# The first and the refilled channel tiles of a two-layer decoder step: order and queues of the start, and one more plain tile in three half layers

## The chip, the core and the metric

The kernel runs on one core of a Trainium2 chip. Its engines are TensorE (in the profile PE for the products and PEld for the weight loads, which overlap them), VectorE (DVE), ScalarE (ACT), GpSimd (POOL) and SyncE (SP). Each takes its instructions in order and waits for others through semaphores. DMAs are issued by SP, ACT and POOL. The metric is the device time of one launch in microseconds (us), as the median of several runs.

## What is computed

The reference is one inference step of a two-layer decoder, for a prompt of 512 tokens and for 8 sample tokens, which the kernel treats as 520 columns that share the weights. Model width D is 1024 (8 channel tiles of 128), the inner width of a feed-forward half is 2816 (22 tiles of 128).

```python
def _swiglu(x, wg, wu, wd):
    return (jax.nn.silu(x @ wg) * (x @ wu)) @ wd
# every layer: x += 0.5*SwiGLU(rms(x)); x += mixer(rms(x)); x += 0.5*SwiGLU(rms(x))
```

The mixer of layer 0 is a causal pooling with four window sizes, that of layer 1 a windowed attention with sinks on keys and values projected once after layer 0. Everything is float32. There are four SwiGLU halves: 0 and 1 around the pooling, 2 and 3 around the attention. They take most of the time.

## The kernel before

**Products in three terms.** A float32 operand is split into a high part in the rounded type of TensorE and the rest: ScalarE writes the high part (`wh`, `xh`, `th`, `hh`), VectorE the rest (`wl`, `xl`, `tl`, `hl`). `mm` (line 406) makes one product of a 128-channel tile as three terms, each in two halves of 260 columns: six matmuls. Weights are stationary, activations move.

**A half layer** is `ffn` (line 556). It walks its 22 inner tiles in parts of 8, 8 and 6. For each tile it makes the gate and the up product, and after each part the down products of that part, which are added to x. A tile is made in one of two ways:

- `plain_tile` (line 463): gate and up over 8 channel tiles, in four weight pieces of four channel tiles: 4 pieces x 4 channel tiles x 6 = 96 matmuls. VectorE makes four `wl`, and three more operations at the end (lines 488, 490 and 243).
- `strassen_tile` (line 499): the same result by seven instead of eight block products, `product` (line 428) at line 435: 7 x 4 x 3 = 84 matmuls. It wants seven weight pieces, two of them sums that VectorE makes (lines 161 and 165) and two accumulated by DMAs that GpSimd issues (lines 155 and 156). And it wants eight more pairs `tt` of sums of channel tiles, made once per half layer by `sums` (line 533), a generator of eight steps.

`NPL` (line 30) says how many tiles at the head of each half layer are plain: 3, 2, 2, 2.

**Hooks.** At the head of a half layer the norm of x isn't known yet. `start_hooks` (line 610) lists what is to be slipped in between: one or two empty hooks, `norm` (the sum of squares over `acc`, line 378, the inverse root on VectorE, and the first step of `sums`), an empty one, `norm_all` (the root spread over all partitions, line 395, then the end of tiles that waited for it), and seven more steps of `sums`: 12 hooks in halves 0 and 1, 11 in half 3. A plain tile takes one hook after each of its four pieces; what is left when the first Strassen tile comes is done all at once ahead of it. Half 2 has six hooks of its own.

**Order.** The kernel is written for a framework that plans each engine's order by a simulated timeline. `later` (line 248) pins an instruction behind the one written before it on its engine; what isn't pinned may be moved. `Weights` (line 95) is the queue of weights: `chunk` is one load into one of three raw buffers, `piece` one split of 128x512; `get` splits the next piece, `prefetch` splits up to five pieces ahead, `load` and `begin` issue the loads, on SP. There are six buffers for split pieces and four double banks of PSUM (`duo`).

**The start** (lines 628 to 676). ACT issues six small loads (gains in five pieces into `grow`, the samples) and two blocks of x; SP issues the other six blocks of x between the first weights. TensorE transposes the 72 gains (line 657) and the samples of all eight channel tiles (line 662), then per channel tile four blocks of x into PSUM (line 666). VectorE or ScalarE copies them into `x[k]` (lines 667, 669, 671), then the pair `xh`, `xl` is made (lines 245, 246). None of the transposes, copies and splits is pinned. The squares of x follow (lines 363 and 367), and `ffn` for half 0 makes its first tile as any other plain tile, piece by piece.

The functions that the change touches, with what calls them:

Of the kernel before, what the change touches and what calls it, by code (L numbers as in the profile page):

```python
# [11 lines left out]
F32 = mybir.dt.float32  # L12
# [8 lines left out]
KT = 8  # L21
# [5 lines left out]
H = TOK // 2  # L27
PARTS = (8, 8, 6)
LAG = 2
NPL = (3, 2, 2, 2)  # L30
HD = 64
NB = SP // P
WINS = (2, 4, 8, 16)
# [61 lines left out]
class Weights:  # L95
# [81 lines left out]
    def _split(self, i):  # L177
        nc = self.nc
        while self.ns <= min(i, len(self.items) - 1):
            it = self.items[self.ns]  # L180
            self.load(it[0])
            self.add_up(it[0])
            src = it[1](self.chunks[it[0]][1])
            n = src.shape[1]
            wh = self.splp.tile([P, 4, P], F32R, tag="wh", name="wh")
            wl = self.splp.tile([P, 4, P], F32R, tag="wl", name="wl")
            dh, dl = wh[:, :n, :], wl[:, :n, :]
            if len(src.shape) == 4:
                dh = dh.rearrange("p k (e d) -> p k e d", e=2)
                dl = dl.rearrange("p k (e d) -> p k e d", e=2)  # L190
            nc.scalar.activation(dh, src, AF.Copy)  # L191
            nc.vector.tensor_tensor(dl, src, dh.bitcast(F32), op=ALU.subtract)  # L192
# [17 lines left out]
def yoco_step(ctx, tc, ins, outs):  # L210
# [18 lines left out]
    def ps():  # L229
        return duo()[:, 0, :]  # L230
# [17 lines left out]
    def later(ins):  # L248

        return tc.keep_in_program_order(ins)  # L250
# [152 lines left out]
    def terms(w, xx):  # L403
        return ((w[0], xx[0]), (w[0], xx[1]), (w[1], xx[0]))

    def mm(w, kk, mov, banks, first, last, halves=(0, 1)):

        for i, (a, b) in enumerate(terms(w, mov)):
            for hf in halves:
                T.matmul(  # L410
                    banks[:, hf, :H],
                    a[:, kk, :],
                    hcols(b, hf),
                    start=(first and i == 0),
                    stop=(last and i == 2),
                )

    def mm_tile(mov, banks, prefetch=True):
        nk = len(mov)
# [43 lines left out]
    def plain_tile(tmp, mov, hs, hooks):  # L463

        pg, pu = duo(), duo()
        for k0 in (0, 4):
            for banks in (pg, pu):
                w = W.get()
                W.prefetch()
                for k in range(k0, k0 + 4):  # L470
                    mm(w, k - k0, mov[k], banks, k == 0, k == KT - 1)
                if hooks:
                    hooks.pop(0)()
        g = tmp.tile([P, TOK], F32, tag="g", name="g")
        t = tmp.tile([P, TOK], F32, tag="t", name="t")
        if not there[0]:
            S.copy(halves(g), pg[:, :, :H])
            S.copy(halves(t), pu[:, :, :H])

            def rest():  # L480
                V.tensor_tensor(g, g, R, op=ALU.mult)
                S.activation(g, g, AF.Silu)
                V.scalar_tensor_tensor(g, t, -1.0, g, op0=ALU.mult, op1=ALU.mult)
                hidden(g, hs)

            copied.append(rest)
        else:
            V.tensor_tensor(halves(g), pg[:, :, :H], halves(R), op=ALU.mult)
            S.activation(t, g, AF.Silu)
            V.scalar_tensor_tensor(halves(g), pu[:, :, :H], -1.0, halves(t), op0=ALU.mult, op1=ALU.mult)  # L490
            hidden(g, hs)
# [61 lines left out]
            split(tt[k + 4], t34)  # L553
            yield

    def ffn(fi, tmp, mov, hooks, tt, tags, after, before_last=None):
# [70 lines left out]

    mov1 = []
    with ff_pool() as tmp:
        grow = tmp.tile([72, P], F32, tag="g", name="grow")  # L630
        nc.scalar.dma_start(grow[0:48, :], norm_g.rearrange("l n (k p) -> (l n k) p", p=P))
        xs = [big.tile([NS, 512], F32, tag=t, name="xs") for t in HH]
        for i in range(2):
            nc.scalar.dma_start(xs[i], x_sample[:, 0, i * 512 : (i + 1) * 512])
        nc.scalar.dma_start(grow[48:56, :], kv_norm_g.rearrange("(k p) -> k p", p=P))
        nc.scalar.dma_start(grow[56:64, :], final_norm_g.rearrange("(k p) -> k p", p=P))
        nc.scalar.dma_start(grow[64:72, :], pool_scale.rearrange("l (k p) -> (l k) p", p=P))
# [4 lines left out]
        xv = x_prompt[0].rearrange("(b p) c -> p b c", p=P)  # L642

        xt = {}
        for c in range(4):
            for b2 in range(2):
                xt[c, b2] = big.tile([P, 2, 256], F32, tag=TT[b2], name="xt")
                eng = nc.scalar if b2 and c < 2 else nc.sync
                later(eng.dma_start(xt[c, b2], xv[:, 2 * b2 : 2 * b2 + 2, c * 256 : (c + 1) * 256]))
            if c in (0, 2):  # L650
                W.begin(2)
        W.load(2)
        mov0, tt = [], {}
        for k in range(KT):
            if k == 0:
                pg = duo()
                T.transpose(pg[:, 0, :72], grow, ident[:72, :72])
                S.copy(gT, pg[:, 0, :72])
                px = pg[:, 1, :]
                for i in range(KT):  # L660
                    o = px[:, i * NS : (i + 1) * NS]
                    T.transpose(o, xs[i // 4][:, (i % 4) * P : (i % 4 + 1) * P], ident[:NS, :NS])
            pk = ps()
            for b in range(NB):
                src = xt[k // 2, b // 2][:, b % 2, (k % 2) * P : (k % 2 + 1) * P]
                T.transpose(pk[:, b * P : (b + 1) * P], src, ident)
            V.tensor_copy(x[k][:, SP:TOK], px[:, k * NS : (k + 1) * NS])
            if k % 2:
                V.tensor_copy(x[k][:, 0:SP], pk)
            else:  # L670
                S.copy(x[k][:, 0:SP], pk)
            z = pair(XX, [P, TOK])
            split(z, x[k], gcol(0, k))
            mov0.append(z)
        for k in range(KT):
            square(k, tmp, "g")

        prep = {}
        sel = cp.tile([P, 34], F32, name="sel")
# [43 lines left out]
                if i % 2:  # L723
                    yield

        ffn(0, tmp, mov0, start_hooks(tmp, 0, tt, 2), tt, HH, deferred(1, tmp, "g", XX, mov1, TW), pool_prep())

    with tc.tile_pool(name="pm", bufs=2) as pm:
        for k in range(KT):
# [591 lines left out]
```

## Time and profile before

| What | Value |
|---|---|
| median of three runs | 1728.08 us |
| lowest and highest | 1722.71 and 1731.19 us |
| the profiled execution, whole | 1729.8 us |
| its span, from the first to the last instruction | 1728.0 us |
| PE busy | 1669.6 us (97%) |
| DVE busy | 1269.1 us (73%) |
| ACT busy | 904.7 us (52%) |
| POOL busy | 146.1 us (8%) |

All durations below come from the profiled execution; its whole time is 1.8 us above its span and 1.7 us above the median. In a row of the timeline the first two numbers are the start and the length in us, then engine, line, operation, what is written and read, how many instructions are merged in the row, and in brackets how long the engine was idle ahead of them and what ended that. A merged row of matmuls ends later than its last issue, since matmuls overlap; the pace is read from the starts. A row of the chain of waits has start, length, engine, tile, line and count. A row of a window has its bounds and length, then busy us and instructions of PE, PEld, DVE, ACT and POOL, the granted TensorE clock, the busy share of the DMA engines and the GB/s that they moved.

### The profile page before, as it was taken

What the parts mean: (1) busy time and instruction counts of PE and PEld (TensorE: products, weight loads), DVE (VectorE), ACT (ScalarE), POOL (GpSimd) and SP (SyncE); (2) the same over time, 40 slices, a digit from 0 to 9 for tenths busy, and PEclk for the clock granted to TensorE, in tenths of its full rate; (3) what the DMA queues carried; (4) which work ended last, traced back from release to release, by engine and by line L of the source; (5) the groups of instructions that cost most, each with busy time, mean ns of one, the idle gap of its engine ahead of it and who ended that gap; (6) DMA issues with size and microseconds to landing.
All of it is one profiled execution on the core that took longest, in us unless ns stands there. A gap on an engine that the chain in (4) does not pass through costs nothing.

```text
span 1728.0 us, 34367 instructions
## 1 busy us (share of the span) xinstructions
PE 1669.6 (97%) x13701; PEld 1654.0 (96%) x13701; DVE 1269.1 (73%) x2454; ACT 904.7 (52%) x1810; POOL 146.1 (8%) x178
## 2 busy tenths in 40 slices
PE   7999999999899999999999999998889999999996
PEld 7999999999899999999999999998779899999996
DVE  6966866877875875887866866878756785785765
ACT  6643634656552643655543634647855653462553
POOL 0101101001001101001101101100000110110100
PEclk9999999999999999999999999999979999999998
DMA  8646746663445845546646746642112465666531
GB/s 204 159 129 141 171 135 144 180 183 75 102 141 132 182 134 135 141 128 145 155 127 141 174 135 141 155 140 50 25 35 73 111 163 144 146 150 159 135 86 51
DMA packets 315872, 227.06 MB, mean 131 GB/s; under 512 B 9265, under 2 KB 290969, under 8 KB 315671
## 3 DMA queue, kind: packets, MB, share of 16 engines
q1 hardware_dynamic: 285872, 174.82, 35.5%
q0 software_dynamic: 23200, 41.82, 14.7%
q10 hardware_dynamic: 6638, 8.23, 1.5%
q8 instruction: 107, 1.75, 0.4%
q14 instruction: 55, 0.44, 0.1%
HBM read 180.89 MB, written 5.04 MB: 108 GB/s over the span
## 4 chain that ended last, share of the span: by engine, by line
PE 67%; DVE 4%; ACT 3%; issue 0%; ACTq 0%; DVEq 0%
PE ps L435 35%; PE ps L410 30%; ACT sm L1034 1%; DVE sm L1019 1%; PE ps L1075 1%; DVE wl L192 1%; PE ps L1159 0%; PE ps L1052 0%; DVE xl L243 0%; ACT xh L242 0%; PE ps L1127 0%; DVE rp L856 0%; ACT wh L191 0%; PE ps L1250 0%; ACT oT L1087 0%
## 5 line engine op out<-in xcount | busy, mean ns | idle before, releaser
L191 ACT ACTIVATE wh<-raw 128x512 fp32r<-128x512 f32 (+1 forms) x742 | 449.6, 621 | 542.8 <-PE ps L410 326.3
L192 DVE TENSOR_TENSOR wl<-raw,wh 128x512 fp32r<-128x512 f32 (+1 forms) x742 | 491.0, 677 | 206.9 <-ACT wh L191 202.2
L435 PE MATMUL ps<-th,wh 128*128 128x260 f32 x1264 | 358.4, 284 | 5.4 <-ACT th L242 3.7
L435 PE MATMUL ps<-tl,wh 128*128 128x260 f32 x1264 | 358.7, 284 | 0.4 <-DVE tl L243 0.4
L435 PE MATMUL ps<-th,wl 128*128 128x260 f32 x1264 | 356.5, 283 | 0.6 <-DVE wl L192 0.5
L410 PE MATMUL ps<-hh,wh 128*128 128x260 f32 x1376 | 282.1, 286 | 4.0 <-DVE mx L1019 3.0
L410 PE MATMUL ps<-hl,wh 128*128 128x260 f32 x1376 | 280.9, 284 | 0.0
L410 PE MATMUL ps<-hh,wl 128*128 128x260 f32 x1376 | 279.4, 283 | 0.0
L435 PEld LDWEIGHTS ps<-th,wh 128*128 128x128 f32 x1264 | 238.9, 189 | 6.7 <-ACT th L242 4.1
L435 PEld LDWEIGHTS ps<-tl,wh 128*128 128x128 f32 x1264 | 239.4, 189 | 1.3 <-DVE tl L243 1.3
L435 PEld LDWEIGHTS ps<-th,wl 128*128 128x128 f32 x1264 | 238.6, 189 | 1.0 <-DVE wl L192 1.0
L410 PEld LDWEIGHTS ps<-hh,wh 128*128 128x128 f32 x1376 | 213.4, 190 | 5.4 <-DVE mx L1019 3.6
L410 PEld LDWEIGHTS ps<-hl,wh 128*128 128x128 f32 x1376 | 215.0, 190 | 0.0
L410 PEld LDWEIGHTS ps<-hh,wl 128*128 128x128 f32 x1376 | 214.0, 189 | 0.0
L435 PE MATMUL ps<-xh,wh 128*128 128x260 f32 x708 | 198.9, 283 | 0.6 <-ACT wh L191 0.6
L435 PE MATMUL ps<-xl,wh 128*128 128x260 f32 x708 | 198.6, 283 | 0.0
L435 PE MATMUL ps<-xh,wl 128*128 128x260 f32 x708 | 194.7, 282 | 1.0 <-DVE wl L192 1.0
L156 POOL DMA_DIRECT2D raw<-raw x79 | 68.4, 866 | 1389.1 <-DVE wl L192 504.7
L589 DVE TENSOR_TENSOR u<-ps,R 128x520 f32<-128x520 f32 x96 | 67.0, 698 | 107.5 <-PE ps L410 107.5
L435 PEld LDWEIGHTS ps<-xh,wh 128*128 128x128 f32 x708 | 133.6, 189 | 1.0 <-ACT wh L191 0.8
L435 PEld LDWEIGHTS ps<-xl,wh 128*128 128x128 f32 x708 | 133.5, 189 | 0.0
L435 PEld LDWEIGHTS ps<-xh,wl 128*128 128x128 f32 x708 | 131.4, 189 | 1.4 <-DVE wl L192 1.4
(237 smaller groups left out, 2845.7 us busy)
## 6 DMA issues: line engine op xcount, KB each, us to landing
raw<-in_ffn_w_gate_dram SPq DMA_DIRECT2D x87, 512.0 KB, 4.1
raw<-in_ffn_w_up_dram SPq DMA_DIRECT2D x87, 512.0 KB, 5.4
raw<-in_ffn_w_down_dram SPq DMA_DIRECT2D x32, 1024.0 KB, 4.9
raw<-raw POOLq DMA_DIRECT2D x79, 256.0 KB, 3.3
S<-in_ffn_w_up_dram SPq DMA_DIRECT2D x79, 256.0 KB, 5.5
S<-raw POOLq DMA_DIRECT2D x79, 256.0 KB, 4.6
raw<-in_ffn_w_down_dram SPq DMA_DIRECT2D x16, 768.0 KB, 6.2
raw<-in_w_q_dram SPq DMA_DIRECT2D x8, 512.0 KB, 6.7
```

The lines of the kernel that those rows point to most:

```text
L156: G.dma_start(blk(raw, 2, 1), blk(raw, 1, 1), accum_op=ALU.add)
L191: nc.scalar.activation(dh, src, AF.Copy)
L192: nc.vector.tensor_tensor(dl, src, dh.bitcast(F32), op=ALU.subtract)
L410: T.matmul(banks[:, hf, :H], a[:, kk, :], hcols(b, hf), start=(first and i == 0), stop=(last and i == 2),)
L435: T.matmul(bank[:, :H], a[:, kk, :], b, start=(not more and kk == 0 and i == 0), stop=(kk == 3 and i == 2), skip_group_check=more,)
L589: V.tensor_tensor(halves(u), banks[m][:, :, :H], halves(R), op=ALU.mult)
L1019: V.tensor_tensor_reduce(out=sm[:, e * 256 : (e + 1) * 256], in0=self.pe[e][:, bi * 256 : (bi + 1) * 256], in1=cst[:, mk : mk + 256], op0= ...
L1034: S.activation(part(i), part(i), AF.Exp, bias=nm[:, i : i + 1], accum_out=den[:, i : i + 1])
L1075: T.matmul(po[:, bi * 256 : (bi + 1) * 256], a, p_[:, kc_], start=(n == 0), stop=(n == 3 * len(kts) - 1),)
```

## The change

It has two parts. **The start** is written anew. The loads are dealt out in a fixed order: ACT takes the gains of the six norms, the samples and the second quarter of x, SP the other three quarters and the weights, POOL the other gains (into a tile of their own, `grow2`, transposed after the squares). Twelve matmuls of ones by ones are issued at the very start, and a small Square on ScalarE. Then every channel tile is transposed, copied and split in an order that is pinned throughout, two channel tiles ahead of the products, and the gate and up products of the first tile are made per channel tile as it comes, not piece by piece. The first tile takes no hooks. **The plain tiles** become 4, 3, 2, 3 instead of 3, 2, 2, 2: so halves 0, 1 and 3 have one more, and in half 0 the first of the four is the one made in the start.

The diff, with the lists of loads shortened:

```diff
-NPL = (3, 2, 2, 2)
+NPL = (4, 3, 2, 3)
...
+        self.pin = lambda ins: ins
...
-            nc.scalar.activation(dh, src, AF.Copy)
-            nc.vector.tensor_tensor(dl, src, dh.bitcast(F32), op=ALU.subtract)
+            self.pin(nc.scalar.activation(dh, src, AF.Copy))
+            self.pin(nc.vector.tensor_tensor(dl, src, dh.bitcast(F32), op=ALU.subtract))
...
+        plain_end(tmp, pg, pu, hs)
+
+    def plain_end(tmp, pg, pu, hs):
+
         g = tmp.tile([P, TOK], F32, tag="g", name="g")
         t = tmp.tile([P, TOK], F32, tag="t", name="t")
...
-                if j < NPL[fi]:
+                if j == 0 and first is not None:
+                    plain_end(tmp, *first, hs)
+                elif j < NPL[fi]:
                     plain_tile(tmp, mov, hs, hooks)
...
+        grow = tmp.tile([48, P], F32, tag="g", name="grow")
+        grow2 = tmp.tile([24, P], F32, tag="g", name="grow2")
+        later(nc.scalar.dma_start(grow, norm_g.rearrange("l n (k p) -> (l n k) p", p=P)))
         xs = [big.tile([NS, 512], F32, tag=t, name="xs") for t in HH]
         for i in range(2):
+            later(nc.scalar.dma_start(xs[i], x_sample[:, 0, i * 512 : (i + 1) * 512]))
+        for b2 in range(2):
+            load_x(nc.sync, 0, b2)
+        W.begin(2)
+        warm = cp.tile([P, 1], F32, name="warm")
+        later(S.activation(warm, ones[:, 0:1], AF.Square))
+        for b2 in range(2):
+            load_x(nc.scalar, 1, b2)
+        for b2 in range(2):
+            load_x(nc.sync, 2, b2)
+        W.load(0)
+        for b2 in range(2):
+            load_x(nc.sync, 3, b2)
+        W.load(2)
+        nc.gpsimd.dma_start(grow2[0:8, :], kv_norm_g.rearrange("(k p) -> k p", p=P))
...
+        pd = duo()
+        for i in range(12):
+            later(T.matmul(pd[:, 1, :P], ones, ones, start=True, stop=True))
+        later(T.transpose(pd[:, 0, :48], grow, ident[:48, :48]))
+        later(S.copy(gT[:, :48], pd[:, 0, :48]))
+
+        def x_tile(k):
+
+            pd = duo()
             for b in range(NB):
                 src = xt[k // 2, b // 2][:, b % 2, (k % 2) * P : (k % 2 + 1) * P]
+                later(T.transpose(pd[:, 0, b * P : (b + 1) * P], src, ident))
+            src = xs[k // 4][:, (k % 4) * P : (k % 4 + 1) * P]
+            later(T.transpose(pd[:, 1, :NS], src, ident[:NS, :NS]))
+            px = pd.rearrange("p b c -> p (b c)")[:, :TOK]
+            xh, xl = pair(XX, [P, TOK])
+            later(S.activation(xh, px, AF.Copy, scale=gcol(0, k)))
             if k % 2:
+                later(S.copy(x[k], px))
             else:
+                later(V.tensor_copy(x[k], px))
+            later(V.scalar_tensor_tensor(xl, x[k], gcol(0, k), xh.bitcast(F32), op0=ALU.mult, op1=ALU.subtract))
+            mov0.append((xh, xl))
+
+        W.pin = later
+        first = duo(), duo()
+        x_tile(0)
+        ws = [W.get()]
+        x_tile(1)
+        ws.append(W.get())
+        for k in range(KT):
+            if k == 3:
+                ws = [ws[0], ws[1], W.get(), W.get()]
+            for o, banks in enumerate(first):
+                mm(ws[k // 4 * 2 + o], k % 4, mov0[k], banks, k == 0, k == KT - 1, pin=later)
+                if not o and k + 2 < KT:
+                    x_tile(k + 2)
+            if k > 4:
+                W.prefetch()
+        W.pin = lambda ins: ins
         for k in range(KT):
             square(k, tmp, "g")
+        pd = duo()
+        T.transpose(pd[:, 0, 48:72], grow2, ident[:24, :24])
+        S.copy(gT[:, 48:], pd[:, 0, 48:72])
```

`mm` takes a function `pin` for its matmuls, and `ffn` a last argument `first`, the two double banks with the products of the first tile.

More of the change, by code (lines that the diff above doesn't have):

```diff
@@ L404, in terms, with mm @@
         return ((w[0], xx[0]), (w[0], xx[1]), (w[1], xx[0]))
-    def mm(w, kk, mov, banks, first, last, halves=(0, 1)):
+    def mm(w, kk, mov, banks, first, last, halves=(0, 1), pin=lambda ins: ins):
         for i, (a, b) in enumerate(terms(w, mov)):
             for hf in halves:
-                T.matmul(
+                ins = T.matmul(
                     banks[:, hf, :H],
@@ L416, in mm @@
                 )
+                pin(ins)
     def mm_tile(mov, banks, prefetch=True):
@@ L554, in sums, with ffn @@
             yield
-    def ffn(fi, tmp, mov, hooks, tt, tags, after, before_last=None):
+    def ffn(fi, tmp, mov, hooks, tt, tags, after, before_last=None, first=None):
         j = 0
@@ L641, in yoco_step @@
         sraw = cp.tile([P, 16], F32, name="sraw")
[L642 to L652, printed above, removed]
@@ L653, in yoco_step @@
-        mov0, tt = [], {}
[L654 to L663, printed above, removed]
+        mov0, tt = [], {}
+        pd = duo()
@@ L724, in pool_prep @@
                     yield
-        ffn(0, tmp, mov0, start_hooks(tmp, 0, tt, 2), tt, HH, deferred(1, tmp, "g", XX, mov1, TW), pool_prep())
+        after = deferred(1, tmp, "g", XX, mov1, TW)
+        ffn(0, tmp, mov0, start_hooks(tmp, 0, tt, 2), tt, HH, after, pool_prep(), first)
     with tc.tile_pool(name="pm", bufs=2) as pm:
```

20 lines of the change are left out of this document (7 added, 13 removed).

## The prediction, made before the change was run

> **What bounds the kernel now.** I read the page first: who is busy, and what the chain of work that ended last is made of.
>
> ```profile
> PE 1669.6 (97%) x13701; PEld 1654.0 (96%) x13701; DVE 1269.1 (73%) x2454; ACT 904.7 (52%) x1810; POOL 146.1 (8%) x178
> ...
> PE 67%; DVE 4%; ACT 3%; issue 0%; ACTq 0%; DVEq 0%
> ```
>
> TensorE is the bound almost everywhere. So a change gains only where TensorE waits or runs slowly, and it pays for every matmul that it adds. Next I looked for the places where TensorE isn't moving at its own pace, in the chain of waits in order of time.
>
> ```profile
> 447.47 1.97 PE ps L435 x6
> 449.48 50.55 PE ps L435 x408
> ...
> 551.62 74.59 PE ps L435 x624
> ...
> 677.81 54.50 PE ps L435 x456
> ...
> 1377.90 50.74 PE ps L435 x408
> ```
>
> The undisturbed pace is 74.59/624 = 0.1195 us a matmul, and 456 of them, as much as six Strassen tiles leave ahead of the down products, take 54.50. The chain begins with VectorE and ScalarE at the first Strassen tile of half 1, and shows them again in half 3. The timeline of TensorE gives the starts there, and those of half 0, which has one plain tile more.
>
> ```profile
> 55.74 0.28 PE L435 MATMUL ps<-xh,wh 128*128 128x260 f32 x1
> 100.24 0.40 PE L410 MATMUL ps<-hh,wh 128*128 128x260 f32 x2
> ...
> 436.38 0.28 PE L435 MATMUL ps<-xh,wh 128*128 128x260 f32 x1
> 447.47 0.80 PE L435 MATMUL ps<-th,wh 128*128 128x260 f32 x2 [2.63 <-ACT th L242]
> ...
> 1366.70 0.28 PE L435 MATMUL ps<-xh,wh 128*128 128x260 f32 x1
> 1428.48 0.40 PE L410 MATMUL ps<-hh,wh 128*128 128x260 f32 x2
> ```
>
> Half 1: the six tiles run from 436.38 to 449.48 + 50.55 = 500.03, or 63.65; **lost: 63.65 - 54.50 = 9.15**. Half 3: 1366.70 to 1428.48, 61.78; **lost: 7.3**. Half 0: five tiles, 372 matmuls ahead of the down products, 44.50 = 372 x 0.1196; **lost: nothing**. TensorE waits for `th`, the sums: hooks that no plain tile had taken are done all at once. Part of the loss is a slow clock behind the waits:
>
> ```profile
> 450.00:452.00 2.00, 2.00 (x11) 2.00 (x10) 1.38 (x2) 1.30 (x4) 0.00 (x0) 0.50 0.08 21
> ...
> 449.86 0.42 PE L435 MATMUL ps<-tl,wh 128*128 128x260 f32 x1
> 452.03 0.42 PE L435 MATMUL ps<-th,wl 128*128 128x260 f32 x1
> ```
>
> At a granted clock of 0.50, the ten matmuls from 449.86 to 452.03 take 0.217 each.
>
> The start is the third place.
>
> ```profile
> 0.74 0.46 SPq L649 DMA_DIRECT2D xt<-in_x_prompt_dram  x1
> 8.16 0.35 PE L657 MATMUL ps<-ident,grow 72*128 72x72 f32 x1 [8.16 <-DMA grow<-in_pool_scale_dram]
> 10.68 5.61 PE L666 MATMUL ps<-ident,xt 128*128 128x128 f32 x26
> 16.05 0.48 PE L410 MATMUL ps<-xh,wh 128*128 128x260 f32 x2
> 27.35 0.40 PE L410 MATMUL ps<-xh,wl 128*128 128x260 f32 x2
> 30.31 1.28 PE L378 MATMUL ps<-ones,acc 128*128 128x1 f32 x10 [2.56 <-DVE acc L367]
> ```
>
> TensorE waits 8.16 for the last of five loads of gains, transposes until 16.05, makes the first tile by 27.75, then waits until 30.31 for the sum of squares, which is late on VectorE.
>
> **The change, part by part.** *Cost of the plain tiles:* 96 matmuls for 84, 12 x 0.1195 = 1.43 each, **4.3 for three**. That is on the path and certain.
>
> *Half 1.* Three plain tiles take all 12 hooks. What is late next? VectorE, by these rows from 411 to 450:
>
> ```profile
> L192 DVE TENSOR_TENSOR wl<-raw,wh 128x512 fp32r<-128x512 f32 x9 | 6.2, 690 | 0.6 <-ACT wh L191 0.5
> L243 DVE TENSOR_TENSOR tl<-t,th 128x520 fp32r<-128x520 f32 x8 | 5.6, 697 | 2.2 <-ACT th L242 2.2
> L367 DVE TENSOR_TENSOR acc<-acc,sq 128x520 f32<-128x520 f32 x7 | 4.9, 698 | 0.4
> L490 DVE SCALAR_TENSOR_TENSOR g<-ps,t 128x520 f32<-128x520 f32 x1 | 0.7, 693 | 0.0
> ```
>
> A plain tile brings it four `wl` and three more, 7 x 0.69 = 4.8, and takes 96 x 0.1195 = 11.5, so 6.7 is free; the waits proper (456 - 408 - 6 = 42 matmuls in the 11.09 from 436.38 to 447.47, less 42 x 0.1195) were 6.1. That is just enough. Half 0 is the better witness: three plain tiles, twelve hooks, nothing lost. Between nothing left and half of the 9.15 left, I take 1.0, since VectorE has little to spare: **9.15 - 1.0 - 1.43 = 6.7 gained** (bounds 3.1 and 7.7).
>
> *Half 3.* It has 11 hooks and its norm comes one piece earlier, so there is more room: 0.4 left, **7.3 - 0.4 - 1.43 = 5.5 gained** (bounds 2.2 and 5.9). The loads and accumulating DMAs that three fewer Strassen tiles spare were waited for by nobody on the path: nothing. Half 2 keeps its two.
>
> *The start.* TensorE: the warm matmuls are 24 passes (a float32 product of ones is two rows, as the 10 for five at line 378). Their price is bounded by the transposes, 0.21 each at the start (26 in 5.37) and 0.11 later:
>
> ```profile
> 809.01 0.45 PE ps L925 x4
> ...
> 0.00:8.00 8.00, 0.00 (x0) 0.00 (x0) 0.18 (x2) 1.28 (x1) 0.70 (x6) 1.00 0.70 213
> 8.00:16.00 8.00, 7.83 (x40) 7.51 (x41) 6.11 (x17) 5.86 (x12) 0.00 (x0) 1.00 1.08 304
> ```
>
> So from about 1.1 they end between 3.8 and 6.3; I take 6.0, as the pace at the start was the slow one. (The clock column says 1.00 there, but twice the time per transpose says half.) By then data are in:
>
> ```profile
> xt<-in_x_prompt_dram SPq DMA_DIRECT2D x6, 256.0 KB, 4.1
> raw<-in_ffn_w_up_dram SPq DMA_DIRECT2D x2, 256.0 KB, 5.1
> grow<-in_norm_g_dram ACTq DMA_DIRECT2D x1, 24.0 KB, 2.7
> ```
>
> The gains land at 0.74 + 2.7 = 3.4, the first quarter of x, issued at 0.74 and some 0.5 later, at 4.8 and 5.3, the first weights behind it, by the same 0.5 an issue, at 6.9 and 7.4. The second quarter stands on ACT's queue behind the table load of the small Square, is issued at about 3.7 and shares the DMA engines with the third. By the two windows 213 x 8 = 1.7 MB are in by 8 and 0.3 more each us: 2 MB by 9, and x with the first tile's weights, 3.1 MB, by 12.7. The second quarter is wanted at 9.5, the rest from 14 on. So how the loads are dealt out is worth nothing by itself, nor costs anything; a quarter that is one us late would cost one. The three loads of `grow2` stand on POOL's queue, and POOL is idle from 8 to 16; its columns are first used after half 0.
>
> Then ScalarE and VectorE, by these rows from 0 to 16:
>
> ```profile
> L658 ACT ACT_TABLE_LOAD x1 | 1.3, 1283 | 6.6 <-DMA raw<-in_ffn_w_up_dram 6.6
> L191 ACT ACTIVATE wh<-raw 128x512 fp32r<-128x512 f32 x4 | 2.4, 627 | 0.0
> L669 DVE COPY x<-ps 128x512 f32<-128x512 f32 x3 | 2.1, 689 | 0.4 <-PE ps L666 0.4
> L246 DVE SCALAR_TENSOR_TENSOR xl<-x,gT,xh 128x520 fp32r<-128x520 f32 x2 | 1.5, 750 | 0.0
> L245 ACT ACTIVATE xh<-x,gT 128x520 fp32r<-128x520 f32 x2 | 1.4, 724 | 0.0
> L363 ACT ACTIVATE sq<-x 128x520 f32<-128x520 f32 x2 | 1.3, 626 | 0.0
> L671 ACT COPY x<-ps 128x512 f32<-128x512 f32 x2 | 1.2, 578 | 1.6 <-PE ps L666 1.6
> ```
>
> Gains transposed and copied by 6.9, `xh` of tile 0 by 7.7, its `wh` by 8.4, `xh` of tile 1 9.1, its copy 9.7, the up piece's `wh` 10.3. VectorE: `xl` of tile 0 8.5, `wl` 9.2, `xl` of tile 1 10.5, the up `wl` 11.2. The up product of channel tile 0 stands ahead of all others on TensorE and waits for that: two matmuls of it (0.24), seven channel tiles at 12 x 0.1195 = 1.43 and the transposes of five, 5 x 0.55 (four at 0.11, a small one), remain: **end at 11.2 + 0.24 + 10.0 + 2.75 = 24.2**. Per channel tile that is 1.43 + 0.55 = 2.0 for TensorE, against 0.72 + half of 0.58 for ScalarE and 0.75 + half of 0.69 for VectorE, and two splits more in the middle: both keep up. Bounds: 23 with no wait for the up piece; 26.5 with all transposes at 0.21; the half clock is a rival below.
>
> Behind it stands the norm, now after three pieces of the second tile, at 24.2 + 8.6 = 32.8. VectorE has by then, from 7 on, four copies (those of line 667 go into them), eight `xl`, twelve `wl` and eight `acc`: 2.8 + 6.0 + 8.3 + 5.3 = 22.4 in 25.8. So the wait of 2.56 goes, if the squares aren't held up; `grow2` shares two buffers with them and must be transposed first. If seven squares wait for that until 24 and then alternate between ScalarE and VectorE in one buffer, 7 x (0.63 + 0.70) = 9.3, they end at 33.5 and the norm waits 1 to 3; I take nothing, as POOL issues those loads at once. So tile and wait end at 24.2 for 30.31, less the 1.43 of the fourth tile: **4.7 gained** (bounds: none, and 6).
>
> *Sum:* 6.7 + 5.5 + 4.7 = 16.9. The profiled execution would take 1729.8 - 16.9 = 1712.9; 1.7 less stands for the median: **1711 us**.
>
> **The rivals.** (a) *The start gives nothing:* the squares come late, or a pinned wait for ScalarE or a load holds the order; 12.2 - 1.4 = 10.8 gained, 1717. For it: every engine waits in order, and a lot stands on my chain of ten steps.
>
> (b) *Slow clock through the first tile.* The first products stand between waits and transposes; if TensorE stays at half speed, 96 matmuls take 0.217 instead of 0.1195, 9.4 more, and the transposes 2.3: 16.9 - 11.7 = 5.2 gained, 1723. For it: the transposes from 8.16 on went at half speed for seven us. Against it: the products at 16.05 went at 0.12 from the first (94 in the 11.30 to 27.35), and a TensorE at half speed has no gaps left. [...]
>
> (c) *Half of the waits at the Strassen tiles stay:* 4.6 and 3.7 left, not 1.0 and 0.4: 6.9 less gained, 1718.
>
> (d) *VectorE, not the hooks, is the bound at all three places.* Then the waits move with the tiles, every one of 9.15, 7.3 and 2.56 stays, the start ends no sooner, and only the 4.3 is left: **1732, slower**. It decides once VectorE has under 6.1 to spare in the added tile; it has 6.7. Against it half 0.
>
> (e) *The plan of order falls otherwise elsewhere.* The attention, seven windows of 24 us from 1158 on with this sum, is planned unpinned.
>
> ```profile
> sum 168.00, PE 151.22 PEld 141.49 DVE 116.42 ACT 107.94 POOL 0.51; mean PE 21.60 PEld 20.21 DVE 16.63 ACT 15.42 POOL 0.07
> ```
>
> TensorE is idle there for 17 already. It would have to lose 26 more to make the kernel slower by 0.5%. The change doesn't touch what it waits for.
>
> **How the numbers follow.** Forecast 0.60 (1705 to 1716), (a) 0.13, (b) 0.07, (c) 0.10, (d) 0.05, (e) 0.05. The range takes in (a), (b), (c) and, below, the whole of the bounds (7.7 + 5.9 + 6 = 19.6) and a run as low as the lowest of before, 5 under the median: 1704 to 1724. A measurement here tells about 0.5%, 8.6 us, from no change. Faster by that is under 1719.4: the forecast, (a), and two thirds of (c), 0.80; within it (b), the rest of (c) and (d), 0.15; slower (e), 0.05.
>
> **What would show it.** Right: the first product at about 8.5, the first tile ended at 24 to 25, no wait at line 378; in halves 1 and 3 six tiles' worth less one, 372 matmuls, in about 45 from the first Strassen product, and no granted clock of 0.50 there. Wrong: gaps behind `th` or `tl` in either half, 0.2 a matmul in the first tile, or a transpose that waits for `xt` or `grow2`.

## The result, and the profile after

| | before | after |
|---|---|---|
| median of four runs | 1726.39 us (1722.71 to 1731.19) | 1711.74 us (1707.83 to 1713.33) |
| the profiled execution, whole | 1729.8 us | 1713.33 us |
| its span | 1728.0 us | 1711.4 us |

The ratio on record is 0.9901, with a 95% interval of 0.9879 to 0.9922: faster by 1.0%, some 17 us (13.5 to 20.9). It is not the quotient of the two medians of the table, which are 14.7 apart; that lies within the interval. The forecast was 1711. Below, the places where that time was to come from are looked at one by one, since a sum can be right by terms that are wrong.

The page of the kernel after, its engines and the shares of the chain:

```profile
PE 1670.1 (98%) x13762; PEld 1655.6 (97%) x13762; DVE 1254.7 (73%) x2422; ACT 899.4 (53%) x1796; POOL 142.5 (8%) x175
...
PE 93%; DVE 4%; ACT 2%; issue 1%; ACTq 0%; DVEq 0%
```

TensorE is as busy as before, in a shorter span. What went is time in which it waited.

**Halves 1 and 3.** The chain of waits of the kernel after, in order of time, at the first parts of these halves and, between them, at an undisturbed part:

```profile
447.12 44.73 PE ps L437 x372
...
543.46 74.68 PE ps L437 x624
...
1368.27 44.45 PE ps L437 x372
```

372 products in 44.73 are 0.1202 each, in 44.45 they are 0.1195, and the undisturbed 624 take 0.1197. VectorE and ScalarE are no longer in the chain there. The timeline of TensorE and a window across the first Strassen tile of half 1 say the same:

```profile
446.95 0.28 PE L437 MATMUL ps<-xh,wh 128*128 128x260 f32 x1
...
491.69 0.40 PE L411 MATMUL ps<-hh,wh 128*128 128x260 f32 x2
```

```profile
436.00:456.00 20.00, 20.00 (x167) 19.84 (x166) 17.47 (x32) 13.48 (x25) 2.62 (x3) 1.00 0.29 54
```

PE is busy for 20.00 of 20 at a granted clock of 1.00, where before there were gaps behind `th` and a clock of 0.50. VectorE, at 17.47 of 20, is close to the next bound.

**The start.** TensorE's waits up to 40 us, with their totals (the row ahead of them is the 1.1 before its first matmul); then its timeline, one row of VectorE, and two windows:

```profile
...
PE ps L411 <- ACT wh L192: 0.6, 1, 0.6
PE ps L411 <- DVE xl L694: 0.5, 1, 0.5
```

```profile
1.06 5.49 PE L675 MATMUL ps<-ones 128*128 128x128 f32 x24 [1.06 <-DVE acc L344]
...
9.16 0.51 PE L411 MATMUL ps<-xh,wh 128*128 128x260 f32 x2 [0.63 <-ACT wh L192]
10.17 0.50 PE L411 MATMUL ps<-xl,wh 128*128 128x260 f32 x2 [0.51 <-DVE xl L694]
10.77 0.80 PE L411 MATMUL ps<-xh,wl 128*128 128x260 f32 x2
...
13.15 0.64 PE L411 MATMUL ps<-xl,wh 128*128 128x260 f32 x2
13.59 0.64 PE L411 MATMUL ps<-xh,wl 128*128 128x260 f32 x2
...
37.10 1.06 PE L379 MATMUL ps<-ones,acc 128*128 128x1 f32 x9
```

```profile
8.62 0.70 DVE L693 COPY x<-ps 128x520 f32<-128x520 f32 x1 [7.60 <-ACT xh L689]
```

```profile
8.00:11.00 3.00, 1.77 (x10) 1.10 (x9) 2.35 (x4) 3.00 (x6) 0.00 (x0) 0.95 1.12 324
11.00:14.00 3.00, 3.00 (x13) 2.65 (x14) 1.94 (x4) 2.07 (x4) 0.00 (x0) 0.50 1.06 318
```

The waits of 8.16 and 2.56 are gone, and no transpose waits for `xt` or `grow2`. But the norm stands at 37.10 instead of the predicted 32.8: between 11 and 14 the granted clock is 0.50, products take 0.22 (two from 13.15 to 13.59), and the chain from the first transpose to the first `wl` is longer than thought. In this execution half 0's first part ends at 99.85, only 0.4 sooner than the 100.24 of before, though with one plain tile more.

So in the two profiles half 1 gives 7.1, half 3 5.8 and the start 0.4, together 13.3 of the 16.5 between the two executions. Most of the other 3.2 lies in the attention (191.55 us from its norm to that of half 3 before, 189.10 after) and around the pool mixer (90.1 from the first of the last down products of half 0 to the norm of half 1 before, 89.1 after). The experiments have to say whether the start is worth 0.4, and whether the 3.2 belong to the change.

### The profile page after: what moved, and what is told of

Same layout as the page of the kernel before. It is cut to its first block, busy times and chain, and to the rows that moved or that the text cites. A ratio compares the mean times of both kernels' runs of the same rounds, so it can differ in the third digit from the quotient of the medians.

```text
span 1711.4 us, 34416 instructions
## 1 busy us (share of the span) xinstructions
PE 1670.1 (98%) x13762; PEld 1655.6 (97%) x13762; DVE 1254.7 (73%) x2422; ACT 899.4 (53%) x1796; POOL 142.5 (8%) x175
## 3 DMA queue, kind: packets, MB, share of 16 engines
q8 instruction: 108, 1.77, 0.4%
## 4 chain that ended last, share of the span: by engine, by line
PE 93%; DVE 4%; ACT 2%; issue 1%; ACTq 0%; DVEq 0%
PE ps L437 45%; PE ps L411 43%; DVE sm L1061 1%; ACT sm L1076 1%; PE ps L791 1%; PE ps L1117 1%; DVE wl L193 1%; PE ps L816 1%; PE ps L379 0%; DVE xl L244 0%; PE ps L1094 0%; PE ps L675 0%; DVE x L598 0%; PE ps L1201 0%; ACT wh L192 0%
## 5 line engine op out<-in xcount | busy, mean ns | idle before, releaser
L437 PE MATMUL ps<-th,wh 128*128 128x260 f32 x1216 | 343.4, 282 | 0.0
L437 PE MATMUL ps<-tl,wh 128*128 128x260 f32 x1216 | 343.0, 282 | 0.0
L437 PE MATMUL ps<-th,wl 128*128 128x260 f32 x1216 | 341.2, 282 | 0.0
L437 PEld LDWEIGHTS ps<-th,wh 128*128 128x128 f32 x1216 | 228.7, 188 | 0.2 <-ACT sa L517 0.2
L437 PEld LDWEIGHTS ps<-tl,wh 128*128 128x128 f32 x1216 | 228.9, 188 | 0.0
L437 PEld LDWEIGHTS ps<-th,wl 128*128 128x128 f32 x1216 | 228.0, 188 | 0.0
L437 PE MATMUL ps<-xh,wh 128*128 128x260 f32 x672 | 188.3, 283 | 0.0
L437 PE MATMUL ps<-xl,wh 128*128 128x260 f32 x672 | 188.1, 282 | 0.0
L437 PE MATMUL ps<-xh,wl 128*128 128x260 f32 x672 | 184.2, 282 | 0.0
L411 PE MATMUL ps<-xh,wh 128*128 128x260 f32 x736 | 149.7, 285 | 0.6 <-ACT wh L192 0.6
L411 PE MATMUL ps<-xl,wh 128*128 128x260 f32 x736 | 149.7, 284 | 0.5 <-DVE xl L694 0.5
L411 PE MATMUL ps<-xh,wl 128*128 128x260 f32 x736 | 148.3, 283 | 0.1
```

Of the source, the lines that this page charges most:

```text
L411: ins = T.matmul(banks[:, hf, :H], a[:, kk, :], hcols(b, hf), start=(first and i == 0), stop=(last and i == 2),)
L437: T.matmul(bank[:, :H], a[:, kk, :], b, start=(not more and kk == 0 and i == 0), stop=(kk == 3 and i == 2), skip_group_check=more,)
```

## The experiments

Three stretches are compared throughout, read from the timeline of TensorE: the end of half 0's first part (its first down product), and for halves 1 and 3 the time from the norm's first matmul to the half's first down product. All in us. A plain tile more is 1.43 of such a stretch.

| kernel | half 0's first part ends | half 1, norm to down | half 3, norm to down | time, us | ratio to before |
|---|---|---|---|---|---|
| before | 100.24 | 77.24 | 79.75 | 1726.39 | |
| after | 99.85 | 70.11 | 73.97 | 1711.74 | 0.9901 |
| e1, plain tiles of halves 1 and 3 alone | 101.80 | 70.03 | 74.15 | 1714.37 | 0.9919 |
| e2, start alone | 97.32 | 76.88 | 78.05 | 1723.69 | 0.9977 |
| e3, after with 3 plain in half 0 | 112.69 | 70.11 | 73.94 | 1726.64 | 0.9993 |
| e4, after without matmuls of ones | 97.80 | 70.11 | 73.96 | 1711.07 | 0.9904 |
| e5, e1 with gains in two tiles | 101.66 | 70.02 | 74.16 | 1713.71 | 0.9911 |
| e6, after with 1 plain in half 2 | 97.26 | 70.11 | 73.97 | 1712.75 | 0.9905 |
| e7, e2 with two hooks per piece, halves 1 and 3 | 97.43 | 79.71 | 75.64 | 1725.03 | 0.9976 |
| e8, e2 with sums partly on GpSimd | 97.45 | 72.10 | 78.78 | 1718.81 | 0.9939 |
| e9, after once more | 97.18 | 70.12 | 73.96 | 1707.93 | one run |
| e10, after a third time | 97.51 | 70.10 | 73.96 | 1708.64 | one run |
| e11, before once more | 103.31 | 76.68 | 79.35 | 1725.38 | one run |
| e12, after with `xl` from PSUM | 99.67 | 70.10 | 73.96 | 1710.23 | 0.9892 |

**Plain tiles alone (e1).** The kernel before with one line changed:

```diff
-NPL = (3, 2, 2, 2)
+NPL = (3, 3, 2, 3)
```

> The kernel before with its old start and 3, 3, 2, 3 plain tiles: one more in halves 1 and 3 alone. Theory (the time came from the waits at the first Strassen tiles of halves 1 and 3, and the new start was worth next to nothing): 7.1 + 5.8 = 12.9 less than before from these two places, first Strassen products of both halves without a gap (372 matmuls in 44.5 to 45), and as good as the whole change, within 2 us, if the attention keeps what it won in the changed kernel; 2 to 3 us behind it if it doesn't. Rival (the prediction's sum, the start worth 4.7): some 5 us slower than the changed kernel.

Ratio 0.9919, interval 0.9899 to 0.9939, which of 1729.22 is 14.0 us (10.5 to 17.5). The two halves give 7.2 and 5.6 in its profile. So the plain tiles of halves 1 and 3 carry most of the result by themselves, and the rival by which VectorE would move the waits along with the tiles falls.

**The start alone (e2).** The kernel after with the last entries set back:

```diff
-NPL = (4, 3, 2, 3)
+NPL = (4, 2, 2, 2)
```

> The changed kernel with 4, 2, 2, 2 plain tiles: the new start and its fourth tile alone. Theory: the start ends no sooner than before once the fourth tile is paid, 0.2 us won by the end of the first Strassen part of half 0, so the time of before within 1 us, and the waits at the first Strassen tiles of halves 1 and 3 back at 9 and 7 us. Rival (prediction): 4.7 us less than before.

Ratio 0.9977, interval 0.9962 to 0.9993: 4.0 us, between 1.2 and 6.6. After the first profile I had come to think that the start gave nothing; this run says otherwise, and the 4.7 of the prediction stands within its interval. The waits of the two halves are there again, in its list of waits for half 1:

```profile
PE ps L437 <- ACT th L243: 2.6, 1, 2.6
PE ps L437 <- ACT wh L192: 1.2, 2, 0.6
...
```

By their points the two parts add up, 14.0 and 4.0 against some 17, though the intervals are wide.

**The first tile without a fourth plain one (e3).** The kernel after with three plain tiles in half 0, the first of which takes no hook:

```diff
-NPL = (4, 3, 2, 3)
+NPL = (3, 3, 2, 3)
```

> The changed kernel with 3 in place of 4 plain tiles in half 0; the first takes no hooks, so four of the twelve are left when the first Strassen tile comes. Theory (what counts is the VectorE work of the sums between the norm and the first Strassen product: 24 to 28 us of time wherever there is no wait): only 17 us lie between, TensorE waits 5 to 9 at the first Strassen tile of half 0, and the kernel is 3.5 to 7.5 us slower than the changed one. Rival (the number of tiles doesn't matter in half 0, as its squares were done early): 1.4 us faster.

It lost 15 to 16 us on the kernel after, twice what I had expected at most, and a part of it ahead of the Strassen tile. Half 0's first part ends at 112.69 instead of 97.2 to 99.9. Its waits between 30 and 115, first TensorE's, then a long one of VectorE, and a window of the half clock:

```profile
PE ps L396 <- DVE r_tok L390: 3.5, 1, 3.5
PE ps L437 <- ACT th L243: 2.1, 1, 2.1
...
```

```profile
DVE raw L162 <- DMA S<-raw: 6.6, 1, 6.6
```

```profile
70.00:77.00 7.00, 6.96 (x32) 6.43 (x32) 4.18 (x7) 3.81 (x10) 0.00 (x0) 0.54 0.37 107
```

VectorE stands for 6.6 on a sum of weights that waits for an accumulating DMA; the inverse root stands behind it in the queue, so TensorE waits 3.5; then four hooks are left when the first Strassen tile comes, TensorE waits there again, and behind the gaps the granted clock is 0.54. So with the new start the fourth plain tile of half 0 isn't decoration: the first tile, made by channel tiles, takes no hooks, and without another one half 0 has a loss like that of halves 1 and 3, and more.

**Without the matmuls of ones (e4).**

```diff
-        for i in range(12):
-            later(T.matmul(pd[:, 1, :P], ones, ones, start=True, stop=True))
```

> The changed kernel without the twelve matmuls of ones. Theory (they hold the first transposes, from 5.3 when x has landed to 6.75, and the clock rose at about 14 whatever ran before): first transpose at about 5.3, first product at about 7.9, the first tile ended 0.5 to 1.3 us sooner. Rival (they bring the clock up sooner: it rose at 14 with them and at 15.4 without in the kernel before): matmuls at 0.21 each until 15.5 or later and the first tile ended at the same time or up to 2 us later.

Ratio 0.9904, interval 0.9884 to 0.9924: the same as after. Without them the transposes begin at 4.13, not at 6.75, and TensorE runs at half pace until about 11.5 (the transposes from 5.99 take 0.26 each); with them it starts later and is faster earlier (in e9, below, 0.15 each from 5.79 on). What the one gives the other takes.

**Only the gains' loads of the start (e5).** e1 with `grow` in two tiles, the second loaded through POOL and transposed after the squares:

```diff
-        grow = tmp.tile([72, P], F32, tag="g", name="grow")
+        grow = tmp.tile([48, P], F32, tag="g", name="grow")
+        grow2 = tmp.tile([24, P], F32, tag="g", name="grow2")
...
-        nc.scalar.dma_start(grow[48:56, :], kv_norm_g.rearrange("(k p) -> k p", p=P))
...
+        nc.gpsimd.dma_start(grow2[0:8, :], kv_norm_g.rearrange("(k p) -> k p", p=P))
...
```

> The old start with 3, 3, 2, 3 plain tiles, with one thing of the new start: the gains of the six norms alone in one tile with one load, the others in a second tile loaded by POOL and transposed after the squares. Theory (the old start lost most by waiting 8.16 for the last of five small loads): transposes from about 5.3, the first product at about 13, and everything behind it 2.5 to 3 sooner than with the old start, so the first Strassen part of half 0 ends at 97 to 98 (100.2 and 101.8 with the old start) and the kernel is level with the changed one. Rival (VectorE's squares set the end of the start, not the transposes): the norm still starts at about 30 and nothing is won over the old start with 3, 3, 2, 3.

Ratio 0.9911, interval 0.9889 to 0.9934, the same as e1, and the first product comes at 16.21 as before. The wait of 8.16 for the gains (they come in four loads, not five as written above) was real, but other waits lay under it. Its timeline of TensorE, and the wait at the norm:

```profile
3.48 0.34 PE L658 MATMUL ps<-ident,grow 48*128 48x48 f32 x1 [3.48 <-POOL ident masks.py:199]
...
8.77 0.69 PE L667 MATMUL ps<-ident,xt 128*128 128x128 f32 x2 [3.67 <-DMA xt<-in_x_prompt_dram]
...
10.34 5.53 PE L667 MATMUL ps<-ident,xt 128*128 128x128 f32 x26
...
16.21 0.51 PE L410 MATMUL ps<-xh,wh 128*128 128x260 f32 x2 [0.18 <-ACT x L672]
```

```profile
PE ps L378 <- DVE acc L367: 2.3, 1, 2.3
```

The gains are there at 3.48, then x is what TensorE waits for, until 8.77; then 26 transposes at half pace (5.53 for all, 0.21 each) stand ahead of the first product; and the wait for the squares, 2.3 here, takes up what is left. So it isn't one load that brings the start's gain. What is left is the order (products between the transposes) together with the way the loads are dealt out; no run tried these two apart.

**One plain tile in half 2 (e6).**

```diff
-NPL = (4, 3, 2, 3)
+NPL = (4, 3, 1, 3)
```

> The changed kernel with 4, 3, 1, 3 plain tiles: one less in half 2, whose sums are mostly made during the key and value products. Theory (a plain tile is worth its 1.43 only where VectorE still has sums to make; in half 2 VectorE is busy about half of the time around the first Strassen tile): no wait appears, 1.4 us less than the changed kernel. Rival (every half layer needs its two): a wait of 3 us or more at the first Strassen product of half 2, and slower by 2 or more.

Ratio 0.9905, interval 0.9888 to 0.9921: no better. From the norm of the keys to that of the attention it takes 375.6 instead of 373.8. A tile's 1.43 is saved and about 3.3 are lost, some 2 of them in new waits around the first Strassen tile of half 2. TensorE waits 2.8 between 795 and 815, where the kernel after waits 0.8:

```profile
PE ps L967 <- ACT vtok L968: 1.2, 1, 1.2
PE ps L437 <- DVE g L494: 0.7, 1, 0.7
...
```

**Hooks placed closer (e7).** e2, with two hooks after each piece in halves 1 and 3 once the norm is known:

```diff
                 if hooks:
+                    hooks.pop(0)()
+                if two[0] and there[0] and hooks:
                     hooks.pop(0)()
...
+        two[0] = fi in (1, 3)
```

> The changed kernel with 4, 2, 2, 2 plain tiles, with two hooks taken per piece in halves 1 and 3 once the norm is known, so that two plain tiles take all hooks. Theory (VectorE hasn't the time for the sums): the waits stay, from the norm to the first down product 75 to 78 us in half 1 and 76 to 80 in half 3, as without it. Rival (the hooks were only placed too late): 68.7 in half 1 and 72.5 in half 3, 12 us or more less than with 4, 2, 2, 2.

Ratio 0.9976, interval 0.9962 to 0.9990, the same as e2. Half 1 takes 79.71, even longer, and half 3 75.64, less than the 78.05 to 79.75 of the other kernels with two plain tiles and old hooks; both lie outside the ranges that I had written down. In half 1 the waits only change their names:

```profile
PE ps L437 <- ACT wh L192: 2.7, 2, 1.5
PE ps L437 <- ACT th L243: 1.7, 1, 1.7
...
```

So in half 1 it isn't that the hooks come too late; the run fits more work for VectorE and ScalarE than two plain tiles have room for. In half 3 the place of the hooks is worth 2.4 to 4.1 in this one profile, where the plain tile brings 5.0.

**Less work for VectorE (e8).** e2, with two of the four kinds of additions in `sums` on GpSimd in halves 1 and 3, eight operations in each:

```diff
-            later(V.tensor_tensor(t1, b11, b12, op=ALU.subtract))
+            if n in (2, 5):
+                nc.gpsimd.tensor_tensor(t1, b11, b12, op=ALU.subtract)
+            else:
+                later(V.tensor_tensor(t1, b11, b12, op=ALU.subtract))
```

(and the same for `t3`).

> The changed kernel with 4, 2, 2, 2 plain tiles, with two of the four additions in each step pair of the sums moved from VectorE to GpSimd in halves 1 and 3: 8 x 0.42 = 3.4 us less for VectorE in each. Theory (VectorE's amount of work is the limit): the waits at the first Strassen tiles get 2 to 4 us shorter in both halves, unless one of GpSimd's additions takes over 1 us. Rival (it is the chain from addition to split and back, not the amount): no shorter, or longer by what GpSimd is slower.

Ratio 0.9939, interval 0.9917 to 0.9960, 5 to 6 us better than e2. Half 1 goes from 76.88 to 72.10 with two plain tiles as before: taking eight additions of 0.42, 3.4 us, off VectorE gives 4.8. An addition takes longer on GpSimd, 0.72 to 1.36 and 0.98 in the mean of six rows from 1339 to 1351, so the chain from addition to split got no shorter; that speaks for VectorE's amount as the bound there. Half 3 stays at 78.78, but not at the sums: from the first Strassen product to the first down product 456 matmuls now take 54.49, 0.1195 each, where e2 has 60.10. The wait has moved to the norm's root. Its waits in half 3, VectorE's rows, and GpSimd's:

```profile
PE ps L396 <- DVE r_tok L390: 1.6, 1, 1.6
PE ps L411 <- ACT R L401: 1.6, 1, 1.6
```

```profile
1344.62 0.15 DVE L390 SCALAR_TENSOR_TENSOR ny<-nt,ny 128x5 f32<-128x5 f32 x1
...
1346.32 0.91 DVE L388 SCALAR_TENSOR_TENSOR nt<-nt,nv 128x5 f32<-128x5 f32 x1
1347.15 0.97 DVE L563 SCALAR_TENSOR_TENSOR t<-t,xb 128x260 f32<-128x260 f32 x1
...
1350.10 0.71 DVE L390 SCALAR_TENSOR_TENSOR r_tok<-nt,ny 128x5 f32<-128x5 f32 x1
...
1351.81 0.43 DVE L563 SCALAR_TENSOR_TENSOR t<-t,xb 128x260 f32<-128x260 f32 x1
```

```profile
1346.47 1.36 POOL L560 TENSOR_TENSOR t<-xb,xa 128x260 f32<-128x260 f32 x1
...
1349.62 1.17 POOL L552 TENSOR_TENSOR t<-xa 128x260 f32<-128x260 f32 x1 [0.96 <-DVE nt L388]
```

The small steps of the root, 0.15 each, stand between large operations of VectorE there, and while GpSimd is busy one of them takes 0.91, another 0.71, and an addition 0.97 instead of 0.43. From 1348 to 1360 TensorE is then busy for 8.80 of 12 with 51 matmuls, at a granted clock of 0.72. A plain tile is the better remedy: 70.1 and 74.0.

**The same kernels again (e9, e10, e11).** No edit.

> The kernel after, unchanged, profiled once more. In its first profile TensorE ran at half pace until 14 us and the first tile's norm came at 37.1; in three other kernels with the same start the half pace ended near 9.8 and the norm came at 34.5 to 34.7. Theory: it is the execution that differs, not the kernel, so the norm may come here at 34.5 to 34.7 with the first Strassen part of half 0 ending near 97.3 instead of 99.85. Rival: the pinned order of this kernel's engines puts something in the way of TensorE at 7 to 14, and the norm comes at 37.1 again, whatever the execution.

> The same once more, to see how far one execution differs from another. Theory (the execution differs): the norm anywhere between 34.5 and 37.2, in step with the time at which the matmuls come to 0.12 us each. Rival (the kernel differs): 37.1, with the pace rising at 14 again.

> The kernel before, unchanged, profiled once more. Its first Strassen part of half 0 ended at 100.24, and with the same start and other plain tiles at 101.80, where TensorE ran at half pace for 1.5 us behind the wait of 2.56 at the norm. Theory: the old start, too, differs by execution, 100.2 to 101.8, and the waits at the first Strassen tiles of halves 1 and 3 come again (77 and 80 us from the norm to the first down product of the second part, within 3). Rival: all at the times of the first profile, within 0.3.

The norm of the kernel after comes at 34.43 and 34.76, not 37.10. The same rows of e9 as shown above of after:

```profile
1.06 4.61 PE L675 MATMUL ps<-ones 128*128 128x128 f32 x24 [1.06 <-DVE acc L344]
...
8.12 0.50 PE L411 MATMUL ps<-xh,wh 128*128 128x260 f32 x2 [0.77 <-ACT wh L192]
8.98 0.50 PE L411 MATMUL ps<-xl,wh 128*128 128x260 f32 x2 [0.36 <-DVE xl L694]
9.59 0.51 PE L411 MATMUL ps<-xh,wl 128*128 128x260 f32 x2
9.94 0.60 PE L684 MATMUL ps<-ident,xt 128*128 128x128 f32 x4
...
11.20 0.40 PE L411 MATMUL ps<-xh,wl 128*128 128x260 f32 x2
...
12.14 0.60 PE L684 MATMUL ps<-ident,xt 128*128 128x128 f32 x4
...
34.43 1.17 PE L379 MATMUL ps<-ones,acc 128*128 128x1 f32 x10
```

```profile
8.00:11.00 3.00, 2.42 (x14) 1.82 (x15) 2.96 (x6) 3.00 (x7) 0.00 (x0) 1.00 1.07 297
11.00:14.00 3.00, 3.00 (x26) 2.81 (x25) 2.12 (x4) 2.01 (x5) 0.00 (x0) 1.00 1.04 316
```

In the same instructions 26 matmuls start between 11 and 14 instead of 13, at 1.00 instead of 0.50. The rival, that the kernel's order is in its own way there, falls. The kernel before differs as well; its rows at the norm, first of e11, then its window:

```profile
30.59 2.29 PE L378 MATMUL ps<-ones,acc 128*128 128x1 f32 x10 [2.57 <-DVE acc L367]
```

```profile
30.00:37.00 7.00, 6.41 (x30) 6.42 (x31) 3.93 (x17) 0.64 (x2) 1.73 (x2) 0.51 0.85 200
```

Half 0's first part ends at 103.31 here, beyond the 101.8 that I had expected at most. Behind the wait of 2.57 TensorE ran at 0.51 here; behind the 2.56 of the first profile it hadn't (57 matmuls in that window instead of 30). From the norm to the end of half 0's first part it took 72.72 here and 69.93 there. e1 and e5, with the same norm behind waits of 2.56 and 2.3, lie between: 71.43 both, and in e1 the products from 32.36 to 35.39 took 0.22 each. So the wait in the old start costs up to 2.8 us more than itself, by the execution. Kernels with exactly the old start end half 0's first part at 100.24, 101.80 and 103.31, mean 101.8; those with exactly the new one (after, e2, e6 to e10) at 97.18 to 99.85, mean 97.7. The difference is **4.1**, as e2's time has it. The attention took 191.55 and 188.3 us in the two profiles of before and 189.1, 186.6 and 186.7 in the three of after, and over all fourteen profiles, none of which changes it, from 184.4 (e12) to 191.55, with 185.4 in e5, which has the old start. It varies by itself by more than what was left over. The stretch around the pool mixer is 88.7 in both e9 and e11. So nothing here says that the 3.2 belong to the change.

**`xl` read from PSUM (e12).**

```diff
+            later(V.scalar_tensor_tensor(xl, px, gcol(0, k), xh.bitcast(F32), op0=ALU.mult, op1=ALU.subtract))
             if k % 2:
                 later(S.copy(x[k], px))
             else:
                 later(V.tensor_copy(x[k], px))
-            later(V.scalar_tensor_tensor(xl, x[k], gcol(0, k), xh.bitcast(F32), op0=ALU.mult, op1=ALU.subtract))
```

> The kernel after, with xl of the start computed from the transposed block in PSUM ahead of the copy into x, so that VectorE's copy is no longer between xh and xl. Theory: VectorE's copy of the first tile only starts when ScalarE is through with the same PSUM tile (8.62 in the profile after), so this takes 0.7 us out of the chain to the first wl: the gate product's third term at about 10.1 instead of 10.77, the first tile ended 0.5 to 0.7 sooner, and the norm too; in the time 0.6 us, too little to tell from none (ratio to the kernel after within 0.997 to 1.002). Rival: TensorE's own work per channel tile sets the end, and only the first product moves: the norm as before this edit for the same pace.

Ratio to before 0.9892, interval 0.9868 to 0.9916: not to be told from after. The chain did not get shorter. Its timeline of TensorE, then one row of ScalarE:

```profile
8.60 0.40 PE L411 MATMUL ps<-xl,wh 128*128 128x260 f32 x2
9.59 0.51 PE L411 MATMUL ps<-xh,wl 128*128 128x260 f32 x2 [0.59 <-DVE wl L193]
...
11.41 0.58 PE L411 MATMUL ps<-xh,wh 128*128 128x260 f32 x2 [0.73 <-ACT wh L192]
```

```profile
10.23 0.59 ACT L692 COPY x<-ps 128x520 f32<-128x520 f32 x1
```

`xl` is in time, but the copy now stands between it and `wl`, so the third term comes at 9.59 as in e9. And ScalarE's copy of the second tile starts at 10.23, when VectorE is through with `xl` of the same PSUM tile, 1.7 later than in e9, so that the up piece's `wh` is late and TensorE waits another 0.73. In this execution the half pace came back from 11.4 on (0.22 a product from 12.73 on, and a granted clock of 0.62 from 11 to 14), and the norm stood at 36.95. No version tried beats the kernel after by more than the measurement tells.

## Why the prediction was right, point by point

- **Half 1:** predicted 6.7. The three profiles with two plain tiles (before, e2, e11) take 76.7 to 77.2, the nine with three and all hooks taken 70.0 to 70.1: 6.9. Right, with its reason: no wait, no slow clock, 372 matmuls in 44.7. Of the 1.0 us of waits that I had left standing, some 0.3 was there (44.73 for 372 matmuls, against 44.45 in half 3). That VectorE is next in line is borne out by e8, and that the place of the hooks isn't the limit here by e7. My opening sentence, that the waits came because the left hooks are done all at once, was too simple for half 1: done sooner, as in e7, they cost as much.
- **Half 3:** predicted 5.5. 78.1 to 79.8 against 73.9 to 74.2: 5.0, and 5.8 in the two profiles. Right; nothing of the 0.4 that I had left standing is there. A part of the gain could be had by placing the hooks otherwise (e7), which the prediction didn't weigh.
- **The start:** predicted 4.7, measured 4.0 by time (1.2 to 6.6) and 4.1 by profiles. With the plain tiles in place the times put it lower: ratios of 0.9919 and 0.9911 with the old start (e1, e5) against 0.9901, 0.9904 and 0.9892 with the new one (after, e4, e12), some 3 us, within the same noise. The size was about right, its working only in part, and that the two agree is partly luck. Right: the waits for gains and for the squares go, no load is late, the first product comes at 8.1 to 9.2 for about 8.5. Wrong: the first norm, 34.4 to 37.1 for 32.8. One term of the sum was too small: a channel tile takes TensorE 2.2, not 2.0. In e9 the transposes start at 9.94, 12.14, and so on; five such tiles make 1.2 of the 1.6 us by which e9's norm is late. I also let VectorE copy a tile while ScalarE makes its `xh`; the row at 8.62 shows that it waits for that. This delays the first `xl`, but not the end: the up product's third term, which I had put at 11.2, starts at 11.20 in e9, and e12, which takes the copy out of the way of `xl`, has the gate product's third term no sooner than e9 (9.59 in both). In the first profile the half clock (0.50 from 11 to 14) adds 2.7. What made up for the shortfall was a term that I didn't have: in three of the four executions with the old start's norm the wait of some 2.5 was paid for again behind it, 1.5 us in e1 and e5, 2.8 in e11, in e1 and e11 with products of 0.22 each.
- **Rival (a),** a start worth nothing, looked true in the first profile and fell with e2 and e9. **Rival (b),** the slow clock, came to a quarter: 2.7 of its 11.7 (37.10 against 34.4), between 11 and 14 in one execution of three, not through the tile. The slow stretch differs by execution: some 3.2 us, from 10.8 to 14.0, in the first profile of after, with a clock of 1.00 there in e9 and e10; some 6.2 us, from 30.6 to 36.8, in e11, with a clock of 1.00 there in the first profile of before. What decided isn't shown by these runs (TensorE was busy for 1.77 and 1.84 of the three us from 8 on where the clock fell, in after and e12, and for 2.42 and 2.10 where it didn't, in e9 and e10; that is a coincidence in four executions, not a tested rule). In e11 nothing but transposes stood ahead of the products, 26 of them from 10.83 on at 0.21 each, and the products from 16.64 on took 0.12 each.
- **Rivals (c) and (d)** fall: no listed wait stays at the Strassen tiles of halves 1 and 3, and e1 gains. **(e)** falls as well: the attention isn't longer.
- **The sum** of 16.9 stands against some 17 (13.5 to 20.9 by the interval) in time and 6.9 + 5.0 + 4.1 = 16.0 by the stretches. Its three parts are right within the noise; in the first two profiles alone, however, it was mostly the attention's chance that filled what the start lacked. The 1711 for the median is closer than the terms deserve.

## What to carry to other kernels

Where an engine that feeds TensorE has too much to do for a stretch, a little more work for TensorE there can pay: in half 1 a tile that costs 1.43 us brought 6.9 net. Before an order is made tighter, ask whether the feeding engine's amount or its order is the limit; in half 1 spreading the hooks did nothing, taking 3.4 us off VectorE gave 4.8. And a stage at the start should be judged by several executions: one profile said 0.4, the mean of several and a time said 4.

## What the runs showed of the hardware that was not expected

- The clock fell back in the same instructions in one execution of after (0.50 from 11 to 14) and not in two others (1.00 in e9 and e10); behind the old start's wait of 2.56 to 2.57 the granted clock from 30 to 37 was 1.00 in the mean (before) and 0.51 (e11), and in e1 the products from 32.36 to 35.39 took 0.22 each.
- At the very start the clock column is 1.00 (0 to 8 us) while 24 passes of the matmuls of ones took 5.42, 0.226 each, in after, and 0.189 in e9. Up there the pace of the matmuls has to be read, not the column.
- GpSimd's subtraction of 128x260 took 0.72 to 1.36 us in e8, 0.98 in the mean of six, VectorE's 0.42 in before and after, and VectorE's operations beside it were up to six times as long (0.15 to 0.91): the 0.91 at 1346.32 stands beside GpSimd's 1.36 at 1346.47.
- Two engines that read one PSUM tile went one after the other in this framework: in after VectorE's copy starts at 8.62, when ScalarE's `xh` of that tile (7.89 and 0.69 long) is done; in e12 ScalarE's copy starts at 10.23, when VectorE's `xl` of that tile (9.45 and 0.75 long) is done.
